# Moving the start of the activation rows from byte 128 to byte 0 of 512 in SBUF

## The chip, the cores and the metric

The kernel runs on one core of a Trainium2 chip. Its time is the device time of one execution in microseconds. Before the change three executions took 1005.29, 1007.73 and 1007.76 us; the median is 1007.73 us.

## The reference, cut to what matters

Two transformer blocks work on 256 tokens of width 1024. The first has a windowed attention and a differential attention, both gated and merged, and then a feed-forward part; the second has a chunked delta rule and a sparse latent attention, then a cross attention over 256 memory rows, and again a feed-forward part. All is float32. The feed-forward part, which takes more time than any other, is

```
gate_up = u @ w_ffn_in[l]
f = (silu(gate_up[..., :D_FF]) * gate_up[..., D_FF:]) @ w_ffn_out[l]
```

with D_FF = 2816. The second one has `w_gate`, `w_up` and `w_down` in place of these. Nearly all other work of TensorE is a projection of the same kind: 256 tokens times a weight matrix of 1024 rows.

## The kernel before, in words

Activations stand with features on the 128 partitions and tokens along the row: a block of 128 features is one row segment of 256 float32 numbers, 1024 bytes in each partition. Every float32 operand of a projection is split into a high and a low part (`split`, L285 to L292 for activations, `load_w` for weights) that TensorE takes at the full rate of the rounded type. `gemm` (L314 on) makes one output block of 128 features: it loads 512 KB of weights, splits them on ScalarE (L309) and VectorE (L311) into `wh` and `wl`, and issues 24 matmuls at L325: for each of eight blocks `wh` with the high and with the low rows, and then `wl` with the high rows. Weights are stationary (128 columns, 512 bytes in a partition, loaded before every matmul while the one before it streams), the rows are moving (256 columns, 1024 bytes). Each matmul has its own weight load.

The moving rows of these matmuls are, in the order of the program:

- `uh`, `ul`: the normalized input of a projection. In the first block's attention (gates, queries, values; 768 matmuls of 256 columns and 240 of 272), in both feed-forward parts (`ffn_in`, 1056 each) and in the queries of the cross attention (192).
- `od_h`, `od_l` and `m_h`, `m_l`: 192 matmuls each, between the attention and the first feed-forward part.
- `mem_h`, `mem_l`: the memory rows, 192 matmuls with the rows moving, 192 (L821 to L823) with the rows stationary and the weights moving.
- `f_h`, `f_l`: the inside of the feed-forward part. In the first block 528 matmuls with the rows moving. In the second (`down`, L1650 to L1654) they are stationary, and the weights `wh`, `wl` move, in pieces of 512 and 256 columns; 330 matmuls.
- `mix_h`, `mix_l` and `ox_h`, `ox_l`: 192 matmuls each, in the two residual steps of the second block.

The tiles get their addresses from an allocator when the program is built. The start of each row segment, counted as its address modulo 512 bytes, is: `u`, `f`, `mix`, `ox`, `od`, `m` 128; `mem` 64; nearly all weights 64 (one of the last three `wh` of the second feed-forward part 192). A row segment of 256 numbers and a weight segment of 128 are whole multiples of 512 bytes, so all blocks of a tile start at the same byte. The table `AT` (L214) holds how many numbers a tile's first row is moved into its allocation; `rows_at`, `new_u_at` and `parts_at` (L415 to L425) use it. In the three `ffn_in` steps j = 3, 6 and 12 a matmul with a stationary block of zeros (L328) stands after the fourth matmul of the gate's `gemm`; it adds nothing to the sum.

The order of the work on each engine comes from a scheduler at build time.

Of the kernel before, what the change touches and what calls it, by code (L numbers as in the profile page):

```python
# [17 lines left out]
F32R = mybir.dt.float32r  # L18
# [7 lines left out]
P = 128  # L26
NT = 256
# [6 lines left out]
FT = FF // P  # L34
# [176 lines left out]
BDLAST = 0  # L211
WARM = 12

AT = {'ffn1': 112, 'xatt': 0, 'ffn2': 112, 'mem_h': 112, 'mem_l': 112, 'mix_h': 0, 'mix_l': 0, 'ox_h': 0, 'ox_l': 0, 'f': 0, 'first': 112}  # L214
RB = 2
MAGIC = float(0x5F3759DF)
SWAP = [i ^ 16 for i in range(32)]
# [4 lines left out]
def _program(tc, d, out):  # L222
# [4 lines left out]
    def new_pool(stack, name, bufs=1, space=None, side=None):  # L227
        kw = {} if space is None else {"space": space}
        if side is not None:
            kw["side"] = side  # L230
        return stack.enter_context(tc.tile_pool(name=name, bufs=bufs, **kw))

    with ctx:
# [189 lines left out]
        def parts_at(pool_, name, at_h, at_l):  # L423
            return [rows_at(pool_.tile([P, KT * NT + P], F32R, name=name + e), at)
                    for e, at in (("_h", at_h), ("_l", at_l))]  # L425
# [12 lines left out]
        uh, ul = ([t[:, at + k * 3 * P:at + k * 3 * P + NK] for k in range(KT)] for t, at in (  # L438
            (gpool.tile([P, KT * 3 * P + 112], F32R, name="u" + e, tag="u" + e), AT["first"] + (0, 16)[e == "l"])
            for e in "hl"))  # L440
# [6 lines left out]
        for k in range(1, KT, 2):  # L447
            n = min(2, KT - k)
# [321 lines left out]
        first = [None]  # L770
# [19 lines left out]
        mem_h = mhp.tile([P, 8, NT], F32R, name="mem_h")  # L790
        mem_l = mhp.tile([P, 8, NT], F32R, name="mem_l")
# [37 lines left out]
        mpool = new_pool(mg, "m")  # L829
# [24 lines left out]
        def post_norm(src_w, xs, gain, res, res_out, g_next, at=0, at_l=0, whole=False):  # L854

            fg = mpool.tile([P, 8, NT], F32, name="fg", tag="fg")
            acc = gpool.tile([P, NK], F32, name="acc", tag="acc", bufs=1)[:, :NT]
            for j in range(8):
                def use(o, j=j):
                    act.activation(fg[:, j, :], o, AF.Copy, scale=G(gain, j))  # L860
                    sumsq(j, o, acc, NT)
                gemm_long(src_w[j], xs, NT, use)
            rr = gpool.tile([P, NK], F32, name="rs", tag="rs", bufs=2)
            rsqrt_of(opool, acc, ones_d, NT, rr[:, :NT])
            if whole:
                u = gpool.tile([P, KT, NK], F32, name="u", tag="uh")
            else:
                uh, ul = new_u_at(at, at_l)
            acc2 = gpool.tile([P, NK], F32, name="acc2", tag="acc2", bufs=1)[:, :NT]
            for j in range(8):  # L870
                dve.tensor_tensor(fg[:, j, :], fg[:, j, :], rr[:, :NT], OP.mult)  # L871
                pool.tensor_tensor(res_out[:, j, :], fg[:, j, :], res[:, j, :NT], OP.add)
                if whole:
                    act.activation(u[:, j, :NT], res_out[:, j, :], AF.Copy, scale=G(g_next, j))
                else:
                    split(uh[:, j, :NT], ul[:, j, :NT], res_out[:, j, :], G(g_next, j))
                sumsq(j, res_out[:, j, :], acc2, NT)
            rs2 = gpool.tile([P, NK], F32, name="rs", tag="rs", bufs=2)
            rsqrt_of(opool, acc2, ones_d, NT, rs2[:, :NT])
            if whole:  # L880
                return [u[:, k, :NT] for k in range(8)], rs2[:, :NT]
            return [(uh[:, k, :NT], ul[:, k, :NT]) for k in range(8)], rs2[:, :NT]

        h1 = rpool.tile([P, KT, NT], F32, name="h1", tag="resB")
        us, rs = post_norm(d["w_out1"], [(m_h[:, k, :], m_l[:, k, :]) for k in range(8)],
                           "post_mix", hT, h1, "pre_ffn", at=AT["ffn1"], at_l=AT["ffn1"] + 16)

        def ffn_in(pool_, src_w, us, rs, f_h, f_l):
            zeros = pool_.tile([96, P], F32R, name="zeros")
            pool.memset(zeros.bitcast(F32), 0.0)  # L890
            for j in range(FT):
                sg = pool_.tile([P, NT], F32, name="sg", tag="sg", bufs=3)

                def use_g(o, sg=sg):
                    dve.tensor_tensor(sg, o, rs, OP.mult)  # L895
                    act.activation(sg, sg, AF.Silu)  # L896
                    pool.tensor_tensor(sg, sg, rs, OP.mult)  # L897

                def use_u(o, sg=sg, j=j):
                    t = pool_.tile([P, NT], F32, name="ft", tag="ft", bufs=2)  # L900
                    dve.tensor_tensor(t, o, sg, OP.mult)  # L901
                    split(f_h[:, j, :], f_l[:, j, :], t)

                bank = lambda i: ppool.tile([P, 512], F32, name="s", tag="s") if 2 * j + i < 3 else None
                gemm(src_w[2 * j], us, NT, use_g, ps=bank(0), zero=zeros if j in (3, 6, 12) else None)
                gemm(src_w[2 * j + 1], us, NT, use_u, ps=bank(1))
            tc.keep_in_program_order(act.preload_act_table_set(EXP_LN))
# [20 lines left out]
        late(cc, d["const_c"])  # L928
        fst = ExitStack()
        mpool = new_pool(fst, "f")  # L930
        f_h = mpool.tile([P, FT, NT], F32R, name="f_h")
        f_l = mpool.tile([P, FT, NT], F32R, name="f_l")
        ffn_in(mpool, d["w_gu1"], us, rs, f_h, f_l)
        s = ppool.tile([P, 512], F32, name="s", tag="s")
        pe.matmul(s[:8, :384], relb, cc, start=True, stop=True)
# [39 lines left out]
        dve.memset(ones_q, 1.0 / 256)  # L975
        mix_h, mix_l = parts_at(bpool, "mix", AT["mix_h"], AT["mix_l"])

# [561 lines left out]
        def residual(src_w, xs, res, res_out, g_next, late=(), more=0, at=0):  # L1539
            uh, ul = new_u_at(at, at)  # L1540
            acc = gpool.tile([P, NK], F32, name="acc", tag="acc", bufs=1)[:, :NT]
            for j in range(8):
                def use(o, j=j):
                    dve.tensor_tensor(res_out[:, j, :], o, res[:, j, :], OP.add)
                    added.append(split(uh[:, j, :NT], ul[:, j, :NT], res_out[:, j, :], G(g_next, j)))
                    sumsq(j, res_out[:, j, :], acc, NT)
                ps = ppool.tile([P, 512], F32, name="s", tag="s") if 2 <= j < 2 + more else None
                gemm(src_w[j], xs, NT, use, ps=ps, late=late if j < 2 + more else ())
            rs2 = gpool.tile([P, NK], F32, name="rs", tag="rs", bufs=2)
            rsqrt_of(opool, acc, ones_d, NT, rs2[:, :NT])  # L1550
            return [(uh[:, k, :NT], ul[:, k, :NT]) for k in range(8)], rs2[:, :NT]

        x2 = rpool.tile([P, KT, NT], F32, name="x2", tag="resB")
        us, rs = residual(d["w_out2"], [(mix_h[:, k, :], mix_l[:, k, :]) for k in range(8)], x1, x2, "g_xattn", (0,1,2,3), 2, AT["xatt"])
        b2.close()
# [7 lines left out]
        def two(name, src):  # L1563
            h, l = (xpool.tile([P, 2, NT], F32R, name=name + e, tag=name + e, bufs=2) for e in "hl")
            with tc.issue_after(added[1].ins):
                act.activation(h, src, AF.Copy)
            pool.tensor_tensor(l, src, h.bitcast(F32), OP.subtract)
            return h, l
        keys = [two("kx_", kx[:, 2 * h:2 * h + 2, :]) for h in range(4)]
        values = [two("vx_", vx[:, :, h * NT:(h + 1) * NT]) for h in range(4)]  # L1570
        ox_h, ox_l = parts_at(xpool, "ox", AT["ox_h"], AT["ox_l"])
        rx = xpool.tile([P, 4], F32, name="rx")
# [45 lines left out]
        x3 = rpool.tile([P, KT, NK], F32, name="x3", tag="resA")[:, :, :NT]  # L1618
        us, rs = residual(d["w_xo"], [(ox_h[:, k, :], ox_l[:, k, :]) for k in range(8)], x2, x3, "g_ffn", (4,5,6,7), 2, AT["ffn2"])
        xa.close()  # L1620
# [4 lines left out]
        mpool = new_pool(fst, "f2")  # L1625
# [4 lines left out]
        for qb in range(2):  # L1630
# [5 lines left out]
        f_h, f_l = (mpool.tile([P, FT * NT + P], F32R, name=n)[:, AT["f"]:AT["f"] + FT * NT].rearrange(  # L1636
            "p (a b) -> p a b", a=FT) for n in ("f_h", "f_l"))
# [31 lines left out]
        for qb in range(2):  # L1669
# [13 lines left out]
            a = mpool.tile([P, 1], F32, name="ra", tag="ra", bufs=2)  # L1683
            b = mpool.tile([P, 1], F32, name="rb", tag="rb", bufs=2)
# [31 lines left out]
```

## Time and profile before

| | |
|---|---|
| median of three executions | 1007.73 us |
| the profiled execution's own time | 1007.77 us |
| its span, first to last instruction | 1005.9 us |
| TensorE busy (PE) | 982.8 us, 98% |
| weight loads (PEld), beside PE | 915.2 us, 91% |
| VectorE (DVE), ScalarE (ACT), GpSimd (POOL) busy | 685.1, 541.3, 222.8 us |
| mean granted TensorE clock | 0.993 |

A matmul's record in this profile is longer than the time that it holds up the next one (the engine is a pipeline): what it costs is the distance from its start to the start of the next. That distance is read from the timeline, or from a piece of the chain of waits, in which a run of matmuls is one row with its duration and count.

### The profile page before, as it was taken

What the parts mean: (1) busy time and instruction counts of PE and PEld (TensorE: products, weight loads), DVE (VectorE), ACT (ScalarE), POOL (GpSimd) and SP (SyncE); (2) the same over time, 40 slices, a digit from 0 to 9 for tenths busy, and PEclk for the clock granted to TensorE, in tenths of its full rate; (3) what the DMA queues carried; (4) which work ended last, traced back from release to release, by engine and by line L of the source; (5) the groups of instructions that cost most, each with busy time, mean ns of one, the idle gap of its engine ahead of it and who ended that gap; (6) DMA issues with size and microseconds to landing.
All of it is one profiled execution on the core that took longest, in us unless ns stands there. A gap on an engine that the chain in (4) does not pass through costs nothing.

```text
span 1005.9 us, 18620 instructions
## 1 busy us (share of the span) xinstructions
PE 982.8 (98%) x7218; PEld 915.2 (91%) x7218; DVE 685.1 (68%) x1466; ACT 541.3 (54%) x1097; POOL 222.8 (22%) x258
## 2 busy tenths in 40 slices
PE   9999999999999999999999899999999999999996
PEld 8888898998988989999999888787799999999885
DVE  6788789788655776656544739967687686566534
ACT  5566657667545755555544444335676554444433
POOL 5534326233230213121100312121021011212002
PEclk9999999999999999999999999999999999999999
DMA  6433333332435465555666232333056155555651
GB/s 238 151 110 104 123 126 106 106 126 87 165 120 194 148 210 199 186 184 187 211 199 195 85 127 84 126 105 105 1 167 203 70 181 185 185 186 189 208 189 64
DMA packets 42023, 149.26 MB, mean 148 GB/s; under 512 B 4728, under 2 KB 5376, under 8 KB 41808
## 3 DMA queue, kind: packets, MB, share of 16 engines
q1 hardware_dynamic: 40896, 145.47, 43.8%
q0 software_dynamic: 608, 2.03, 0.7%
q8 instruction: 56, 0.92, 0.4%
q10 hardware_dynamic: 432, 0.59, 0.2%
q14 instruction: 31, 0.25, 0.1%
HBM read 147.01 MB, written 1.06 MB: 147 GB/s over the span
## 4 chain that ended last, share of the span: by engine, by line
PE 57%; DVE 9%; ACT 2%; issue 1%; ACTq 0%; DVEq 0%
PE mm L325 36%; PE mm L341 4%; PE s L325 2%; PE ac L1653 2%; PE ac L1654 2%; PE ac L1650 2%; DVE wl L311 1%; DVE fg L871 1%; PE mm L1413 1%; PE mm L823 1%; DVE ul L292 1%; PE mm L821 1%; PE mm L822 1%; DVE y L1014 1%; DVE base L1158 0%
## 5 line engine op out<-in xcount | busy, mean ns | idle before, releaser
L311 DVE TENSOR_TENSOR wl<-raw,wh 128x1024 fp32r<-128x1024 f32 (+1 forms) x232 | 285.0, 1229 | 101.1 <-ACT wh L309 94.3
L309 ACT ACTIVATE wh<-raw 128x1024 fp32r<-128x1024 f32 (+1 forms) x232 | 242.8, 1048 | 175.0 <-PE mm L325 100.9
L325 PE MATMUL mm<-uh,wh 128*128 128x256 f32 (+1 forms) x1040 | 257.6, 284 | 0.0
L325 PE MATMUL mm<-ul,wh 128*128 128x256 f32 (+1 forms) x1040 | 255.8, 282 | 0.4 <-DVE ul L292 0.4
L325 PEld LDWEIGHTS mm<-uh,wh 128*128 128x128 f32 x1040 | 195.3, 188 | 2.8 <-ACT wh L309 0.6
L325 PEld LDWEIGHTS mm<-ul,wh 128*128 128x128 f32 x1040 | 195.3, 188 | 1.2 <-DVE ul L292 0.8
L325 PE MATMUL mm<-uh,wl 128*128 128x256 f32 (+1 forms) x1040 | 152.2, 283 | 0.0
L325 PEld LDWEIGHTS mm<-uh,wl 128*128 128x128 f32 x1040 | 134.6, 188 | 0.8
L341 PE MATMUL mm<-u,raw 128*128 128x256 f32 (+1 forms) x464 | 109.3, 386 | 0.0
L897 POOL TENSOR_TENSOR sg<-sg,rs 128x256 f32<-128x256 f32 x44 | 50.7, 1154 | 232.1 <-ACT sg L896 232.1
L341 PEld LDWEIGHTS mm<-u,raw 128*128 128x128 f32 x464 | 85.5, 190 | 14.0 <-issue 0.9
L901 DVE TENSOR_TENSOR ft<-mm,sg 128x256 f32<-128x256 f32 x42 | 17.8, 424 | 50.8 <-PE mm L325 49.6
L325 PE MATMUL mm<-f_h,wh 128*128 128x256 f32 x176 | 42.5, 279 | 0.0
L325 PE MATMUL mm<-f_l,wh 128*128 128x256 f32 x176 | 42.5, 279 | 0.0
L895 DVE TENSOR_TENSOR sg<-mm,rs 128x256 f32<-128x256 f32 x40 | 16.9, 423 | 32.2 <-PE mm L325 32.2
L288 ACT ACTIVATE f_h<-ft 128x256 fp32r<-128x256 f32 x44 | 18.3, 417 | 38.1 <-DVE ft L901 38.1
L1653 PE MATMUL ac<-wh,f_l 128*128 128x512 f32 (+1 forms) x110 | 38.3, 349 | 0.0
L1650 PE MATMUL ac<-wh,f_h 128*128 128x512 f32 (+1 forms) x110 | 38.3, 348 | 0.0
L1654 PE MATMUL ac<-wl,f_h 128*128 128x512 f32 (+1 forms) x110 | 38.0, 349 | 0.0
L896 ACT ACTIVATE sg<-sg 128x256 f32<-128x256 f32 x44 | 18.1, 417 | 33.4 <-DVE sg L895 33.4
L325 PEld LDWEIGHTS mm<-f_l,wh 128*128 128x128 f32 x176 | 33.0, 188 | 0.0
L325 PEld LDWEIGHTS mm<-f_h,wh 128*128 128x128 f32 x176 | 33.0, 188 | 0.0
(545 smaller groups left out, 2104.7 us busy)
## 6 DMA issues: line engine op xcount, KB each, us to landing
raw<-w_gu SPq DMA_DIRECT2D x88, 512.0 KB, 4.1
raw<-w_dn SPq DMA_DIRECT2D x22, 512.0 KB, 4.3
raw<-w_pr SPq DMA_DIRECT2D x20, 512.0 KB, 3.4
raw<-w_gate SPq DMA_DIRECT2D x16, 512.0 KB, 3.5
raw<-w_out SPq DMA_DIRECT2D x16, 512.0 KB, 3.6
raw<-w_fo SPq DMA_DIRECT2D x16, 512.0 KB, 3.5
raw<-w_kb SPq DMA_DIRECT2D x8, 512.0 KB, 3.5
raw<-w_vb SPq DMA_DIRECT2D x8, 512.0 KB, 3.5
```

What stands on the lines that cost most here:

```text
L288: m = act.activation(h, src, AF.Copy)
L309: act.activation(h[:, :kt * c], raw[:, :kt * c], AF.Copy)
L311: eng.tensor_tensor(l[:, :kt * c], raw[:, :kt * c], h[:, :kt * c].bitcast(F32), OP.subtract)
L325: pe.matmul(o, w[:, k * P:(k + 1) * P], xs[k][i], start=(first and n_ == 0), stop=(last and n_ == len(steps) - 1))
L341: pe.matmul(o, raw[:, k * P:(k + 1) * P], x, start=(k == 0), stop=(k == len(xs) - 1))
L895: dve.tensor_tensor(sg, o, rs, OP.mult)
L896: act.activation(sg, sg, AF.Silu)
L897: pool.tensor_tensor(sg, sg, rs, OP.mult)
L901: dve.tensor_tensor(t, o, sg, OP.mult)
L1650: m = pe.matmul(o, f_h[:, k, tok], h[:, cols], start=(k == 0), stop=False)
L1653: pe.matmul(o, f_l[:, k, tok], h[:, cols], start=False, stop=False)
L1654: pe.matmul(o, f_h[:, k, tok], l[:, cols], start=False, stop=(k == FT - 1))
```

## The change

The table `AT` gets new numbers, and the tiles `f_h` and `f_l` of the first block get the same form as those of the second: a tile that is 128 numbers longer, whose rows begin `AT["f"]` numbers into it. With the allocator's addresses, which stay where they were, every row segment of `u`, `f`, `mix` and `ox` now begins at byte 0 of 512. Rows of `od`, `m` and `mem` and all weights begin where they did. The number and the order of the instructions on each engine are the same before and after.

```
-AT = {'ffn1': 112, 'xatt': 0, 'ffn2': 112, 'mem_h': 112, 'mem_l': 112, 'mix_h': 0, 'mix_l': 0, 'ox_h': 0, 'ox_l': 0, 'f': 0, 'first': 112}
+AT = {'ffn1': 80, 'xatt': 96, 'ffn2': 80, 'mix_h': 96, 'mix_l': 96, 'ox_h': 96, 'ox_l': 96, 'f': 96, 'first': 80}
...
-        f_h = mpool.tile([P, FT, NT], F32R, name="f_h")
-        f_l = mpool.tile([P, FT, NT], F32R, name="f_l")
+        f_h, f_l = (mpool.tile([P, FT * NT + P], F32R, name=n)[:, AT["f"]:AT["f"] + FT * NT].rearrange(
+            "p (a b) -> p a b", a=FT) for n in ("f_h", "f_l"))
```

## Rows read from the trace of the kernel before

**Rows 1.** The page: busy time of each engine, share, instructions; granted clock in tenths

```profile
PE 982.8 (98%) x7218; PEld 915.2 (91%) x7218; DVE 685.1 (68%) x1466; ACT 541.3 (54%) x1097; POOL 222.8 (22%) x258
...
PEclk9999999999999999999999999999999999999999
```

**Rows 2.** PE by stage: stretch, its length, busy (records), granted clock, DMA

```profile
0.00:312.00 312.00, 307.32 (x2146) 1.00 0.40 133
...
396.00:548.00 152.00, 152.00 (x1293) 1.00 0.60 193
...
816.00:936.00 120.00, 120.00 (x1020) 1.00 0.57 185
```

**Rows 3.** The chain of waits: start us, us, what, how many

```profile
375.55 3.38 PE mm L325 x28
...
379.04 16.96 PE mm L325 x144
396.13 33.92 PE mm L325 x288
430.16 118.25 PE mm L325 x1004
...
846.48 33.92 PE mm L325 x288
880.52 56.06 PE mm L325 x476
```

**Rows 4.** Timeline of PE, mix rows: start us, us, line, operation, out<-in

```profile
729.08 0.28 PE L325 MATMUL mm<-mix_h,wh 128*128 128x256 f32 x1
...
729.99 0.62 PE L325 MATMUL mm<-mix_h,wl 128*128 128x256 f32 x4
```

**Rows 5.** Timeline of PE, mem rows

```profile
339.08 0.28 PE L325 MATMUL mm<-mem_h,wh 128*128 128x256 f32 x1
...
341.00 1.12 PE L325 MATMUL mm<-mem_h,wl 128*128 128x256 f32 x8
```

**Rows 6.** Timeline of PE, second block's down stage, f stationary

```profile
941.30 0.28 PE L1650 MATMUL ac<-wh,f_h 128*128 128x256 f32 x1
...
942.01 0.39 PE L1650 MATMUL ac<-wh,f_h 128*128 128x512 f32 x1
...
944.11 0.28 PE L1650 MATMUL ac<-wh,f_h 128*128 128x256 f32 x1
...
944.79 0.39 PE L1650 MATMUL ac<-wh,f_h 128*128 128x512 f32 x1
```

**Rows 7.** Timeline of PE, u rows, beginning of the first ffn_in

```profile
375.70 0.28 PE L325 MATMUL mm<-ul,wh 128*128 128x256 f32 x1
...
377.40 1.07 PE L325 MATMUL mm<-uh,wl 128*128 128x256 f32 x8
```

**Rows 8.** The chain of waits from 333 to 380 us: the matmul with zeros

```profile
378.93 0.12 PE mm L328
```

**Rows 9.** Groups of PE by shape: record's mean length in ns last before the bar

```profile
L325 PE MATMUL mm<-f_h,wl 128*128 128x256 f32 x176 | 24.6, 279 | 0.0
...
L325 PE MATMUL mm<-mem_h,wl 128*128 128x256 f32 x64 | 9.0, 283 | 0.0
...
L325 PE MATMUL mm<-mix_h,wl 128*128 128x256 f32 x48 | 6.7, 276 | 0.0
```

**Rows 10.** The page: weight splits (group, mean ns), and the weights' DMA

```profile
L311 DVE TENSOR_TENSOR wl<-raw,wh 128x1024 fp32r<-128x1024 f32 (+1 forms) x232 | 285.0, 1229 | 101.1 <-ACT wh L309 94.3
L309 ACT ACTIVATE wh<-raw 128x1024 fp32r<-128x1024 f32 (+1 forms) x232 | 242.8, 1048 | 175.0 <-PE mm L325 100.9
...
raw<-w_gu SPq DMA_DIRECT2D x88, 512.0 KB, 4.1
```

**Rows 11.** Waits of PE: who waited for whom, us in total, times, longest

```profile
PE mm L823 <- DVE wl L311: 4.5, 2, 3.9
```

## The prediction

> **What bounds the kernel now.** I read the page first. TensorE is busy for 98% of the span and its clock stands in the page's top tenth in all 40 slices [rows 1], so neither a cold clock nor an idle TensorE leaves much to win. Then the waits of TensorE: the longest sum is 4.5 us, two waits for VectorE's split of a memory weight [rows 11]. Then the stages: TensorE is busy for 307.32 of the first 312 us, and for every microsecond from 396 to 548 and from 816 to 936 [rows 2]. The chain of waits confirms it: there it is one unbroken run of matmuls at L325 [rows 3]. In these stretches the kernel's time is the number of matmuls times the distance between two starts. A change that alters neither number nor order of instructions can act only through that distance.
>
> So I asked what the distance is. In the feed-forward parts it is 118.25 us / 1004 = 117.78 ns, and 33.92 us / 288 = 117.78 ns in both blocks, to the hundredth [rows 3]. These are `u` and `f` rows at byte 128 with weights at byte 64. The same shape runs at other rates elsewhere:
>
> - `mem` rows, byte 64 like the weights: 16 distances from 339.08 to 341.00 us, 120.0 ns [rows 5].
> - `mix` rows, byte 128: eight distances from 729.08 to 729.99 us, 113.8 ns, and nearer 113.3 if more are counted (the times are rounded to 10 ns) [rows 4].
> - `u` rows at the start of the first `ffn_in`: 15 distances from 375.70 to 377.40 us, 113.3 ns [rows 7]. Then comes the matmul with zeros, a stationary block at another place [rows 8], and the next 144 take 16.96 us, 117.8 ns each [rows 3].
>
> The lengths of the records say the same: 276, 279 and 283 ns for `mix`, `f` and `mem` [rows 9]. So with 64 bytes between rows and weights two rates are stable, 113.3 and 117.8 ns. A run keeps its rate until something interrupts it, and what begins or interrupts it chooses. With 0 bytes between them I see only 120.0. [...]
>
> [...]
>
> **The change part by part.** Moved are the rows of 3 x (1024 + 80) = 3312 `u` matmuls, 528 `f`, 192 `mix` and 192 `ox`: 4224 in all. They go from 64 bytes ahead of the weights to 64 bytes behind them. The trace has no moving row at byte 0 with weights at byte 64 in a long run. The nearest rows with 64 bytes behind are those of the second block's down stage, where the weights move (byte 64) and `f` is stationary (byte 128). In its runs of six matmuls of 256 columns both rates appear in turn: from 941.30 to 942.01 us six take 0.71 us, 118 ns, and from 944.11 to 944.79 us six take 0.68 us, 113 ns [rows 6]. [...] That is my nearest row: the same two rates, about as often the one as the other, none above.
>
> What a full move to the fast rate is worth: 117.78 - 113.33 = 4.45 ns a matmul.
>
> - First feed-forward part: 1056 + 528, less 27 that are fast already [rows 7]: 1557. Second: 1056. All on the unbroken chain: 2613 x 4.45 ns = 11.6 us.
> - First attention: (768 + 240) x 4.45 ns = 4.5 us. TensorE is busy there but shares the time with work that waits for VectorE and ScalarE, so I count half as reaching the end, 2.2 us.
> - Cross attention: 192 `u` + 192 `ox`, 384 x 4.45 ns = 1.7 us, counted by half likewise, 0.9 us.
> - `mix`: fast already; nothing to win, and 192 x 4.45 ns = 0.9 us to lose.
> - Down stage: the pair turns round, 64 behind becomes 64 ahead. Its nine pieces of 512 columns take 2.10 us (942.01 to 944.11), 233 ns each [rows 6]. I count it as nothing; if its 132 matmuls of 256 columns went all fast or all slow it would be 132 x 2.2 ns = 0.3 us either way.
>
> All fast: 11.6 + 2.2 + 0.9 = 14.7 us, or 17.8 us if nothing in the attentions is hidden, which gives 1007.8 - 17.8 = 990.0 us, the lower end. From the down stage I take half of 14.7 us, 7.35, less half of the loss of `mix`, 0.45: 6.9 us. All this is counted against the profiled execution, 1007.77 us with a span of 1005.9; it lies 0.04 us from the median of the three runs. 1007.8 - 6.9 = 1000.9; I say 1000.9 us. The half is not a mean over thousands of draws: the two long stretches are one run of matmuls each, so I expect mostly one rate in each of them, and a step of about 7 us (first) or 4.7 us (second) where it is the fast one.
>
> What follows behind a faster TensorE has room: in 24 x 113.3 ns = 2.72 us a `gemm` needs 1.05 us of ScalarE and 1.23 us of VectorE for its weights, and 512 KB in 2.72 us is 193 GB/s, which the stretch from 396 to 548 us moves already [rows 2]; a load lands in 4.1 us with three buffers [rows 10].
>
> **The rivals.**
>
> *All slow.* The new place has the same two rates, but the beginnings choose the slow one everywhere. For it: with 64 bytes ahead that is what both long stretches do, and only `mix` and a few short runs do otherwise [rows 3, 4]. Against it: the down stage takes turns. `mix` loses 0.9 us and the fast 27 lose 0.1: 1008.8 us, no change that can be told.
>
> *No effect of the place.* The rates are a matter of timing alone; then the same beginnings choose the same rates: 1007.8 us. Against it stand the 120.0 ns that `mem` has throughout [rows 5]. [...]
>
> [...]
>
> **How the numbers follow.** What a measurement can tell from no change here is 0.3%, 3.0 us. Forecast, some of the long stretches fast: 0.52, with its own range 990 to 1004.7 us. All slow 0.17 and no effect 0.09: together 0.26 for no change. Meeting at once, or another rate over 118.9: 0.22, from 1010.8 to 1018 us. The range that leaves out two in ten goes from 991 us, just above the lower end, to 1013 us, into the third rival.
>
> **What would show it.** Right: the runs of L325 in the chain from 379 to 548 us and from 829 to 936 us at 113.3 ns a matmul, in one of them at least; records of 276 ns in the groups of `f` or `u`; the `mem`, `od` and `m` groups as before. The down stage shows whether the pair turned round keeps its two rates. [...] I would be wrong altogether if a fourth rate appeared, below 113 or over 121 ns, or if the time changed where no rows were moved.

## The result, and the profile after

The kernel with the moved rows takes 993.4 us (median of four executions, 991.37 to 994.63), the kernel before 1007.75 us in the same comparison: ratio 0.9859, interval [0.9834, 0.9884]. A second comparison gave 993.32 us (five executions), ratio 0.9855 [0.9832, 0.9879]. So the change wins 14.4 us where I had forecast 6.9.

The page of the profiled execution (991.37 us, span 989.5 us) has the busy times and the granted clock in tenths, as [rows 1]:

```profile
PE 966.0 (98%) x7218; PEld 899.2 (91%) x7218; DVE 685.9 (69%) x1466; ACT 541.8 (55%) x1097; POOL 223.2 (23%) x258
...
PEclk9999999999999999999999899999999999999999
```

TensorE is busy for the same share of a shorter span; instructions and the other engines' work are what they were. The chain of waits through the second feed-forward part answers to the row of 288 at 846.48 us in [rows 3]; its columns are start, length, what, how many:

```profile
834.42 32.66 PE mm L325 x288
```

32.66 us / 288 = 113.4 ns from start to start, where it was 117.78. In the first feed-forward part the timeline shows the same; the rows are the eight matmuls of `wl` that end a `gemm`, and one matmul with zeros:

```profile
374.68 1.07 PE L325 MATMUL mm<-uh,wl 128*128 128x256 f32 x8
...
388.28 1.07 PE L325 MATMUL mm<-uh,wl 128*128 128x256 f32 x8
...
389.64 0.29 PE L328 MATMUL mm<-ul,zeros 96*128 96x256 f32 x1
...
391.14 1.07 PE L325 MATMUL mm<-uh,wl 128*128 128x256 f32 x8
...
393.86 1.07 PE L325 MATMUL mm<-uh,wl 128*128 128x256 f32 x8
```

From 374.68 to 388.28 us are five `gemm`s, 120 matmuls in 13.60 us: 113.3 ns. The `gemm` with the zeros takes 2.86 us, the next one 2.72 again. Before the change the first of these matmuls ended the 113.3 ns for good [rows 7, 8]; now the rate survives it. By tile (count, record length in ns as min/median/max, first and last start), the rows of `f`:

```profile
L325 PE MATMUL mm<-f_h,wl x176: 276/276/276, 478.3 to 536.2; 128*128 128x256 f32 x176
```

The same view of `m`:

```profile
L325 PE MATMUL mm<-m_h,wl x64: 276/276/276, 310.7 to 328.9; 128*128 128x256 f32 x64
```

And of `mix`:

```profile
L325 PE MATMUL mm<-mix_h,wl x48: 281/281/281, 717.5 to 737.4; 128*128 128x256 f32 x48
```

`f` went from 279 to 276 [rows 9], the length that goes with 113.3 ns. But `mix`, 276 before [rows 9], is now at 281, 117.8 ns from start to start, and `m`, whose place did not change, is at 276 where it was 279. The down stage, as in [rows 6]:

```profile
939.51 0.28 PE L1650 MATMUL ac<-wh,f_h 128*128 128x256 f32 x1
...
940.20 0.39 PE L1650 MATMUL ac<-wh,f_h 128*128 128x512 f32 x1
...
942.25 0.28 PE L1650 MATMUL ac<-wh,f_h 128*128 128x256 f32 x1
...
942.93 0.39 PE L1650 MATMUL ac<-wh,f_h 128*128 128x512 f32 x1
```

Every run of six now takes 0.68 to 0.69 us, where 0.71 and 0.68 took turns, and nine pieces of 512 columns take 2.05 us, 228 ns each (228.9 over more of them), where they took 233.

Where the time came from, by the starts of stages in three profiled executions (us; the second profile after is e12 below). The long run of an `ffn_in` is its part without a gap; 120 of the first one's 1056 matmuls and 44 of the second one's stand ahead of it.

| stretch | before | after | after, second profile |
|---|---|---|---|
| start to first matmul of `m` | 306.0 | 304.5 | 305.3 |
| from there to the long run of the first `ffn_in` | 69.4 | 65.4 | 67.7 |
| from there to the last `f` matmul | 172.7 | 166.4 | 166.4 |
| from there to the next block's first run of 32 matmuls at L341 | 27.3 | 28.0 | 28.5 |
| from there to the long run of the second `ffn_in` | 241.3 | 241.4 | 241.2 |
| from there to the end | 189.2 | 183.8 | 183.8 |
| span | 1005.9 | 989.5 | 992.7 |

The long feed-forward stretches are shorter by a fixed amount, 6.3 and 5.4 us, and the first attention by 0.8 to 1.6. The second and the fourth line differ between the two executions of the same kernel, and the granted clock (the number behind TensorE's busy time and its records) shows why. First the second line, before, after and second profile (columns as in [rows 2]):

```profile
306.00:375.40 69.40, 66.10 (x512) 0.95 0.57 189
...
304.50:369.80 65.30, 62.26 (x512) 1.00 0.63 201
...
305.30:372.90 67.60, 64.54 (x512) 0.97 0.61 194
```

And the fourth:

```profile
548.20:575.40 27.20, 23.34 (x166) 0.94 0.29 98
...
536.30:564.20 27.90, 24.05 (x166) 0.88 0.30 97
...
539.30:567.70 28.40, 24.54 (x167) 0.88 0.30 95
```

By half microseconds, the granted clock in these stretches is 0.50 in place of 1.00 for some time: before the change from 313.5 to 316.5, 358.0 to 361.0 and 566.0 to 569.0 us, in the first profile after it from 552.5 to 559.0 us. Ahead of each TensorE waits (it is busy for 0.50 of the 2 us from 310.0, 0.86 of those from 354.0, 0.01 of those from 562.0 and, after the change, 0.10 of those from 550.0), but not every wait brings it: after the change TensorE is busy for 0.82 of the 2 us from 350.0, and the clock stays at 1.00. In the second line that can cost up to 69.4 x 0.05 = 3.5 us before the change, 67.6 x 0.03 = 2.0 in the second profile after, and nothing in the first (estimates from these rows): of the 4.0 and 1.8 us that are gone there, up to 3.5 and 1.5 come from the clock and not from the change. In the fourth the same matmuls keep TensorE busy 0.7 and 1.2 us longer, and by just that the stretch grew; the 8 among the nines of the page stands for it.

### The profile page after: what moved, and what is told of

It is laid out like the page before. It is cut to its first block, busy times and chain, and to the rows that moved or that the text cites. A ratio compares the mean times of both kernels' runs of the same rounds, so it can differ in the third digit from the quotient of the medians.

```text
span 989.5 us, 18620 instructions
## 1 busy us (share of the span) xinstructions
PE 966.0 (98%) x7218; PEld 899.2 (91%) x7218; DVE 685.9 (69%) x1466; ACT 541.8 (55%) x1097; POOL 223.2 (23%) x258
## 5 line engine op out<-in xcount | busy, mean ns | idle before, releaser
L325 PE MATMUL mm<-uh,wh 128*128 128x256 f32 (+1 forms) x1040 | 251.7, 282 | 0.0
L325 PE MATMUL mm<-ul,wh 128*128 128x256 f32 (+1 forms) x1040 | 249.5, 280 | 0.8 <-DVE ul L292 0.8
L325 PEld LDWEIGHTS mm<-uh,wh 128*128 128x128 f32 x1040 | 195.5, 188 | 2.8 <-ACT wh L309 0.6
L325 PEld LDWEIGHTS mm<-ul,wh 128*128 128x128 f32 x1040 | 195.7, 188 | 1.4 <-DVE ul L292 1.0
L325 PE MATMUL mm<-uh,wl 128*128 128x256 f32 (+1 forms) x1040 | 148.9, 280 | 0.0
L325 PEld LDWEIGHTS mm<-uh,wl 128*128 128x128 f32 x1040 | 131.7, 188 | 0.8 <-issue 0.2
L341 PE MATMUL mm<-u,raw 128*128 128x256 f32 (+1 forms) x464 | 109.3, 386 | 0.0
L341 PEld LDWEIGHTS mm<-u,raw 128*128 128x128 f32 x464 | 85.5, 190 | 14.0 <-issue 0.9
L325 PE MATMUL mm<-f_l,wh 128*128 128x256 f32 x176 | 41.1, 276 | 0.0
L325 PE MATMUL mm<-f_h,wh 128*128 128x256 f32 x176 | 41.1, 276 | 0.0
L514 POOL TENSOR_TENSOR ropem<-rawq,cqt 128x256 f32<-128x256 f32 x16 | 18.9, 1179 | 64.6 <-ACT rawq L511 64.5
L325 PEld LDWEIGHTS mm<-f_l,wh 128*128 128x128 f32 x176 | 33.0, 188 | 0.0
```

Of the source, the lines that this page charges most:

```text
L325: pe.matmul(o, w[:, k * P:(k + 1) * P], xs[k][i], start=(first and n_ == 0), stop=(last and n_ == len(steps) - 1))
L341: pe.matmul(o, raw[:, k * P:(k + 1) * P], x, start=(k == 0), stop=(k == len(xs) - 1))
L514: pool.tensor_tensor(m[:, :n], raw[:, :n], c, OP.mult)
```

## The experiments

In the expectations, distance is the start of the moving rows less that of the stationary block: before the change 64 (ahead), after it -64 (behind). Theory A: the place sets the odds with which a run of matmuls takes one of two rates, and the run keeps its rate until something interrupts it. Theory B: the place alone decides. Theory C: the timing of the beginning alone.

| run | what | us | ratio to before |
|---|---|---|---|
| e1 | rows at byte 64 | 1015.19 | 1.0092 [1.0062, 1.0122] |
| e2 | only `u` at byte 0 | 996.69 | 0.9901 [0.9879, 0.9924] |
| e3 | zero matmul's block taken from `w` | 1006.75 | 1.0001 [0.9984, 1.0017] |
| e6 | rows at byte 256 | 991.12 | 0.9845 [0.9823, 0.9866] |
| e7 | after, `mem` at byte 0 too | 991.25 | 0.9853 [0.9831, 0.9875] |
| e8 | after, run of `mix` broken | 993.74 | one execution |
| e9 | only `f` at byte 0 | 1007.85 | 0.9993 [0.9978, 1.0009] |
| e10 | e9, run of `f` broken | 1005.08 | one execution |
| e11 | e7, run of `mix` broken | 990.87 | 0.9841 [0.9818, 0.9863] |
| e12 | after, again | 993.32 | 0.9855 [0.9832, 0.9879] |

### e1: the rows at the same byte as the weights

```
-AT = {'ffn1': 80, 'xatt': 96, 'ffn2': 80, 'mix_h': 96, ... 'f': 96, 'first': 80}
+AT = {'ffn1': 96, 'xatt': 112, 'ffn2': 96, 'mix_h': 112, ... 'f': 112, 'first': 96}
```

> The kernel after with the rows of u, f, mix and ox at byte 64, the byte at which the weights begin. Three theories. A (place sets the odds): with a given distance between rows and weights certain rates are stable, a run keeps its rate until something interrupts it, and the distance sets which rate its beginning falls into. B (place alone): each distance has one rate, whatever went before. C (timing alone): the place is indifferent. A and B expect 120.0 ns a matmul in both long stretches, as the mem rows have it at this distance, and about 1018 us (4032 matmuls x 2.2 ns and 192 x 6.7 ns over 1007.8). C expects 113.3 or 117.8 ns and 991 to 1008 us.

It took 1015.19 us. The stretches of the first and second feed-forward part (columns: stretch, length, PE busy with its number of records, granted clock, DMA share, GB/s) show fewer matmuls at the same clock:

```profile
400.00:430.00 30.00, 30.00 (x252) 1.00 0.58 190
...
840.00:900.00 60.00, 60.00 (x502) 1.00 0.58 185
```

The changed kernel has 267 and 531 records in these stretches. Less the two or three in flight at the edges, 252 in 30 us are 120.0 ns each. So 120.0 ns a matmul was right for distance 0, though the time stayed 2.8 us under the 1018 us expected; 64 behind, the changed kernel's long runs have 113.4. C is out: with the same beginnings the place moved the time by 21.8 us.

### e2: `u` alone

```
-... 'mix_h': 96, 'mix_l': 96, 'ox_h': 96, 'ox_l': 96, 'f': 96, ...
+... 'mix_h': 0, 'mix_l': 0, 'ox_h': 0, 'ox_l': 0, 'f': 0, ...
```

> Only the rows of u begin at byte 0; f, mix and ox are back at byte 128. A: gates and ups of both feed-forward parts at 113.4 ns as after; the f run of the first part follows without an interruption and keeps 113.3 ns although its rows lie at byte 128; the second part's down stage takes turns again (six in 0.685 and 0.707 us); about 994.5 us. B: u at 113.4 ns, f and ox back at 117.8 ns, mix at 113.3 ns: 993.4 + 528 x 4.45 ns + 192 x 4.45 ns - 192 x 4.45 ns + 1 = 996.8 us. C: any mixture of the two rates.

It took 996.69 us. `u` runs at 113.5 ns; `f`, 64 ahead as before the change, is at 117.8 from its first matmul, right behind `u` at 113.5:

```profile
L325 PE MATMUL mm<-f_h,wl x176: 278/280/281, 481.5 to 541.7; 128*128 128x256 f32 x176
```

B's number held, in part by luck: it counted `mix` at 113.3 ns, and `mix` ran at 117.8 here (median record 280 ns). A's, that 113.3 ns go on at the other distance, did not: `f` at 64 ahead dropped them at the border, though nothing stands between.

### e3: does the zero block's place end the 113.3 ns?

```
-                    pe.matmul(o, zero, xs[k][i][:96], start=False, stop=False)
+                    pe.matmul(o, w[:96, k * P:(k + 1) * P], xs[k][i][:96], start=False, stop=False)
```

> The kernel before (rows at byte 128) with one thing changed: the six extra matmuls at L328 take their stationary block from the weights at byte 64 (96 of their rows) in place of the block of zeros at byte 256 or 128; so what they add to the sum is not zero. Order and count of instructions stay. A: the first of them no longer interrupts the fast run that begins at 375.5 us; the first feed-forward part keeps 113.3 ns, 1557 x 4.45 ns = 6.9 us less: 1000.9 us; the second part, which begins slow, stays slow. If it is not the block's place but its 96 rows that interrupt, or under B, nothing changes: 1007.8 us.

In this kernel, the one before but for that block (which adds to the sum, as the zeros did not), the timeline at the first extra matmul reads:

```profile
376.41 1.07 PE L325 MATMUL mm<-uh,wl 128*128 128x256 f32 x8
...
377.77 0.28 PE L328 MATMUL mm<-ul,wh 96*128 96x256 f32 x1
...
379.31 1.10 PE L325 MATMUL mm<-uh,wl 128*128 128x256 f32 x8
```

Eight matmuls of `wl` take 1.07 us before it, 1.10 behind it, as before the change. So A's expectation failed: that it is another matmul ends the run, not where its block lies. And `mix`, at 113.3 ns in the kernel before (276 in [rows 9]), ran at 117.8 ns here with nothing of it changed: the first sign that its rate is drawn anew.

```profile
L325 PE MATMUL mm<-mix_h,wl x48: 277/279/281, 727.5 to 747.4; 128*128 128x256 f32 x48
```

### e4: the distances by themselves

A program of matmuls alone: for each of twelve distances twelve runs of 40, each run behind a float32 matmul of another width.

```
for diff in (-256, -192, -128, -96, -64, -32, 0, 32, 64, 96, 128, 192):
    for e in range(64, 256, 16):
        matmul(st[:, :e], one[:, :P], one[:, :e])
        for n in range(40):
            matmul(acc[:, :256], block n % 8 of wts, block n % 8 of rows)   # rows start diff bytes after wts
```

> A kernel that does none of the reference's work and measures the disputed cost alone: weights at byte 64, rows at twelve distances from them (-256, -192, -128, -96, -64, -32, 0, 32, 64, 96, 128, 192 bytes, in this order), at each twelve runs of 40 matmuls of 128 x 256 of the rounded type, eight blocks in turn; ahead of each run a float32 matmul of 64 to 240 columns, so that the runs begin at different phases. A: 120.0 ns at distance 0; at +64 both 113.3 and 117.8 ns with most runs slow, at -64 both with most runs fast; elsewhere unknown. B: one rate at each distance, 117.8 at +64, 113.3 at -64, 120.0 at 0. C: the same rates at every distance.

One run of 40 of six of the distances from the chain (-256, -192, -64, 0, 64 and 192; start, length):

```profile
60.17 4.79 PE acc L258 x40
...
120.32 4.71 PE acc L258 x40
...
299.41 4.56 PE acc L258 x40
...
419.74 4.79 PE acc L258 x40
...
539.38 4.71 PE acc L258 x40
...
719.19 4.56 PE acc L258 x40
```

-64 and 192 have the shortest, 4.56 / 40 = 114.0 ns with the longer first distances in it and 113.33 behind them; 64 and -192 have 4.71, 117.8; 0 and -256 have 4.79, 120.0 behind the first. The other six take 4.67 to 4.79. Distances 256 apart agree, -128 and 128 (4.75 both) too. At -64 all twelve runs settle at 113.33, at 64 all twelve at 117.78; there the place alone decided, and the even odds of my forecast are gone. Not so everywhere: at -96 the runs settle at 117.2 to 120.0 ns, and at -128 and 128 single ones at 120.1 and the others at 118.8.

### e5: beginnings, orders and other bytes

A second program of this kind; its core, for each of -64 and 64:

```
for c in (31, 45, ... 241):                     # 16 runs of 40 that wait for VectorE
    tensor_copy(o32[:, :c], acc[:, :c]); run(40)
for g in range(6): gemm order, wts/wts2 with rows/rows2, unbroken
for weights at byte 128, 192, 320: 3 runs of 32
for g in range(8): down order: 9 of 512 columns, 6 of 256, two stationary blocks in turn (a, b, a)
```

> A program that does none of the reference's work: only matmuls of 128x256 (and some of 128x512) with a weight load each, clocked by their starts. It asks whether the rate belongs to the distance between the start of the moving rows and that of the weights alone. Theory P (the distance alone, as the first such program showed: 64 bytes behind 113.3 ns, 64 ahead 117.8 ns, whatever comes before): (1) 32 runs of 40 that each begin after a wait for VectorE of another length: 113.3 at 64 behind in all 16, 117.8 at 64 ahead in all 16; (2) the order of a gemm, each weight block twice and two tiles of rows, six gemms unbroken: the same two rates; (3) weights at bytes 128, 192 and 320 with the rows 64 behind or ahead: the same two rates; (4) the order of the down stage, in which each matmul has another stationary block and the moving operand stays for two: the same two rates in its six-runs of 256, so 64 behind 113.3 and 64 ahead 117.8. Theory Q (something else of the sequence decides, as `mix`, 64 behind, runs at 117.8 in the changed kernel, and the down stage, 64 ahead there, at 113.3): some of the 16 runs after a wait go to the other rate, or the order of the down stage turns the two round.

From the chain, four runs that began after a wait (the first two at -64, the next two at 64), the `gemm` order (-64, then 64) and the down order (-64, then 64):

```profile
38.27 4.99 PE acc L262 x40
...
69.79 4.82 PE acc L262 x40
...
133.12 4.99 PE acc L262 x40
...
165.61 4.82 PE acc L262 x40
...
181.53 16.40 PE acc L279 x144
...
198.10 17.01 PE acc L279 x144
...
286.14 22.39 PE acc L294 x120
...
308.69 21.99 PE acc L294 x120
```

After a wait both rates appear at both distances: 4.99 us is a run that settled at 117.8 ns, 4.82 one at 113.3 (the first two intervals, in which it starts up, take 0.34 us). At -64, 13 of 16 settle at 113.3 ns (of the other three, the program's first took 7.05 us), at 64 3 of 16. In the `gemm` order -64 has 113.3 ns and 64 117.8; at other bytes of the weights 8 of 9 and 0 of 9 have 113.3. Over both programs, -64 settles at 113.3 ns in 34 of 38 beginnings (12, 13, 1 and 8) and 64 in 3 of 38. So P's rule is a matter of odds, as A has it, but far from even.

The odds belong to these programs and to how a run begins. Behind another matmul -64 took 113.3 ns in 21 of 22 beginnings and 64 in none of 22; behind a wait it was 13 and 3 of 16. In the kernels the six extra matmuls of L328 agree: behind each of them `u` has 113.3 ns in the seven profiles with `u` at -64 or 192 (after, e2, e6, e7, e8, e11, e12) and 117.8 in the four at 64 (before, e3, e9, e10). Two beginnings don't agree. The first 28 of the long run of the first `ffn_in` have 113.3 ns at 64 too, in all four profiles [rows 7]. And `mix`, which begins behind a wait, has 113.3 ns in one of five profiles at 64 (before; not e2, e3, e9, e10) and in one of five at -64 or 192 (e12; not after, e6, e7, nor e8 ahead of its break): its distance made no difference.

The down order turns it round: at 64 its runs of six are all at 113.3 ns, at -64 they take turns at 113.3 and 117.7 by the starts of single records, just as in [rows 6], in all eight rounds, the same each time. What I had read as odds is the pattern of another order. (Its three matmuls have two stationary blocks, a, b, a; the expectation's "another stationary block" for each doesn't hold between the third and the next.)

### e6: byte 256

```
-AT = {'ffn1': 80, 'xatt': 96, 'ffn2': 80, 'mix_h': 96, ... 'f': 96, 'first': 80}
+AT = {'ffn1': 16, 'xatt': 32, 'ffn2': 16, 'mix_h': 32, ... 'f': 32, 'first': 16}
```

> The rows of u, f, mix and ox begin at byte 256 of 512, 192 ahead of the weights. If the places repeat every 256 bytes, as 192 ahead and 64 behind both ran at 113.3 ns in the program that measured the distances, this is the changed kernel again: 993.4 us, first and second feed-forward part at 113.4 ns. If what counts is nearness in a segment of 512 bytes (rows and weights within 64 bytes or not), 192 ahead has nothing to do with 64 behind in a kernel whose tiles take turns, and the time lies anywhere between 993 and 1015 us.

991.12 us, and the changed kernel's number of records in the same stretch:

```profile
400.00:430.00 30.00, 30.00 (x267) 1.00 0.59 193
```

192 ahead is as good as 64 behind, in the kernel too: with the four pairs of e4, all that was tried speaks for the distance modulo 256 bytes.

### e7: the memory rows as well

```
-        mem_h = mhp.tile([P, 8, NT], F32R, name="mem_h")
+        mem_h = rows_at(mhp.tile([P, KT * NT + P], F32R, name="mem_h"), 112)
```

(and `mem_l` alike.)

> The changed kernel with the memory rows, too, at byte 0 (they were at byte 64, like the weights): 192 matmuls in which they move should go from 120.0 to 113.3 ns, 1.3 us; 192 in which they are stationary and the weights move come to 64 bytes ahead: 117.8 ns by the program that measured the distances (0.4 us), 113.3 by the down stage of the changed kernel (1.3 us). From 993.4 us that makes 990.8 to 991.7 us if nothing else is late there; if VectorE's split of the weights, for which TensorE waits 3.9 us in that stage, takes it back, 993.4 us.

```profile
L325 PE MATMUL mm<-mem_h,wl x64: 276/276/383, 333.5 to 361.4; 128*128 128x256 f32 x64
L821 PE MATMUL mm<-wh,mem_h x64: 276/279/469, 540.3 to 653.9; 128*128 128x256 f32 x64
```

The median is 276 where the rows move (283 in [rows 9]) and 279 where they are stationary (L821; 283 before): the rule carries over to rows that the change left alone. The time, 991.25 us, is within the spread of the changed kernel's executions; a gain of 1.7 us can't be told from none.

### e8: break the run of `mix`

The fourth matmul of three of its `gemm`s is done in two halves:

```
-                pe.matmul(o, w[:, k * P:(k + 1) * P], xs[k][i], ...)
+                for c in ((slice(0, P), slice(P, n)) if cut and n_ == 3 else (slice(0, n),)):
+                    pe.matmul(o[:, c], w[:, k * P:(k + 1) * P], xs[k][i][:, c], ...)
```

> The changed kernel; in the residual step with mix, three of the eight gemms (the third, fifth and seventh) do their fourth matmul in two halves of 128 columns, which breaks the run of equal matmuls. In the changed kernel mix runs at 117.8 ns, 196 matmuls in a row, though its rows stand 64 bytes behind the weights. Theory A, as it now stands (the distance sets the odds with which a run takes one of two rates, here about nine to one for 113.3, and it keeps the rate until something interrupts it): mix goes to 113.3 ns after the first break or the second, and stays there; up to 0.7 us. Rival D (something of mix itself, the place of its weights or of its sums, makes it slow): 117.8 ns after all three breaks, and the time as that of the changed kernel.

```profile
726.09 0.63 PE L326 MATMUL s<-mix_h,wl 128*128 128x256 f32 x4
...
727.50 0.63 PE L326 MATMUL s<-mix_h,wl 128*128 128x256 f32 x4
...
729.74 0.33 PE L326 MATMUL mm<-mix_l,wh 128*128 128x128 f32 x2
...
731.35 1.07 PE L326 MATMUL mm<-mix_h,wl 128*128 128x256 f32 x8
...
734.07 1.07 PE L326 MATMUL mm<-mix_h,wl 128*128 128x256 f32 x8
```

The statement of L325 stands on L326 in this kernel. Ahead of the break twelve matmuls take 1.41 us (117.5 ns), behind it 24 take 2.72 (113.3), and so it stays to the end of `mix`. D is out, and what A says of a break holds in this execution; the nine in ten that it names for a beginning are not what `mix` shows (e5).

### e9 and e10: `f` alone, and its run broken

e9 is the kernel before with the longer `f` tiles of the change and

```
-AT = {... 'f': 0, ...}
+AT = {... 'f': 96, ...}
```

e10 adds the halves of e8 to three of the output blocks of `f`:

```
-                gemm_long(src_w[j], xs, NT, use)
+                gemm_long(src_w[j], xs, NT, use, cut=whole and j in (1, 3, 5))
```

> Only the f rows of the first block, and with them the stationary f of the down stage, begin at byte 0; u, mix and ox stay at byte 128. If the distance decides for each kind of rows by itself: f at 113.3 ns, 528 x 4.45 = 2.3 us; the down stage, whose moving weights then stand 64 ahead of f, as in the changed kernel, at 113.3 and 228.9 ns, 0.7 + 0.3 = 1.0 us; u as before; sum 3.3 us, 1003.0 us against 1006.3. If f takes the rate over from u, which runs at 117.8 ns before it: only the down stage gains, 1005.3 us.

> The kernel in which f alone begins at byte 0, with three matmuls of its first-block product (the fourth of the second, fourth and sixth output block) done in two halves of 128 columns. With f alone moved, f ran at 117.8 ns from its first matmul on, though it stands 64 bytes behind the weights; just before it u runs at 117.8 ns without a gap. Theory A (a run keeps the rate that it entered with, until something breaks it; at 64 behind a new beginning takes 113.3 about nine times in ten): 117.8 ns for 69 matmuls, then 113.3 ns from the first break or the second on, 450 matmuls x 4.45 ns = 2.0 us. Rival D (something of f itself, once u stands elsewhere): 117.8 ns throughout.

e9 took 1007.85 us. Its `f`, 64 bytes behind the weights, is at 117.9 ns, entered straight from `u` at that rate (24 matmuls from row to row: 2.83 us):

```profile
493.01 1.10 PE L325 MATMUL mm<-f_h,wl 128*128 128x256 f32 x8
...
495.84 1.10 PE L325 MATMUL mm<-f_h,wl 128*128 128x256 f32 x8
```

In e10 the same `f` has 117.8 ns for its first 69 matmuls and 113.3 from the first break on:

```profile
491.77 0.87 PE L326 MATMUL mm<-f_h,wl 128*128 128x256 f32 x6
...
492.83 0.33 PE L326 MATMUL mm<-f_l,wh 128*128 128x128 f32 x2
...
494.42 1.07 PE L326 MATMUL mm<-f_h,wl 128*128 128x256 f32 x8
...
497.14 1.07 PE L326 MATMUL mm<-f_h,wl 128*128 128x256 f32 x8
```

So the good place alone isn't enough: a stretch at 117.8 ns keeps that on it until it is broken. Of the two readings of e9 the second held, without even its 1.0 us from the down stage: that runs at the changed kernel's distance, but entered from `u` at 117.8 ns its six-runs stay at 118.0 ns and its 512-column pieces at 230.2, by the starts of single records. With the same distance as in the changed kernel, what stands before the stage differs, and so does its rate.

### e11 and e12: all together, and the change once more

e11 is e7 with two halves in `mix`; e12 the changed kernel itself.

> The changed kernel with mem at byte 0 as well and with two breaks (a matmul in two halves) in the first and the fifth gemm of the step with mix: the sum of what the runs so far point to. mem as in the run with mem alone; mix at 113.3 ns from the first break on, up to 0.8 us. Against the changed kernel in the same call: 1 to 2.5 us less, if nothing else is late there.

> The changed kernel once more, on the same chip as the run before it: 993.4 us, and the second comparison with the kernel before. Every theory expects the rates of the first profile in the two feed-forward parts (113.4 ns); mix and m, which start after a wait, may have taken the other rate.

990.87 and 993.32 us on one chip, 989.67 to 993.40 and 989.88 to 994.59: the difference points the expected way and isn't settled. In e11 the rates are as expected: 276 ns of record for the moving rows of `mem` and for `mix`, in the median. In e12, the same program as the changed kernel, two tiles took the other rate than in the first profile:

```profile
L325 PE MATMUL mm<-m_h,wl x64: 278/279/281, 311.6 to 330.4; 128*128 128x256 f32 x64
```

That is `m`, back at 279; and `mix`, back at 276:

```profile
L325 PE MATMUL mm<-mix_h,wl x48: 276/276/277, 721.1 to 740.2; 128*128 128x256 f32 x48
```

Both begin behind a wait. What they draw differs from execution to execution; `u` and `f` had 113.3 to 113.5 ns in both.

## Why the prediction had the direction right and the size wrong

**What bounds the kernel** was right: number and order of instructions stayed, the mean granted clock nearly so (0.993 before, 0.995 and 0.993 after), and the time went by the distance of two starts.

**Two rates, and a run keeps its rate until something interrupts it**: right, shown by e8 and e10, where a break alone changes the rate, and by e12 against the first profile. One limit: 117.8 ns passed from `u` to `f` (e9), 113.3 ns at 64 behind did not pass to `f` at 64 ahead (e2).

**The failed step is "From the down stage I take half of 14.7 us".** The down stage was the only place with 64 bytes behind [rows 6], but there the weights move and the stationary blocks come in another order. Its two rates take turns by that order (e5), not by even odds. In the order of a `gemm`, e5 has 113.3 ns at 64 behind, unbroken, and in e4 and e5 together 34 of 38 beginnings of all kinds have it. Both long runs went wholly to 113.4 ns, not half of them: 10.7 us where the half had 5.8, and the time moved by 14.4 us in place of 6.9.

**The other terms.** That my sum for "all fast", 14.7 us, comes so near to 14.4 is partly luck, since its terms missed both ways. The long runs: 11.6 us counted, 6.3 + 4.4 = 10.7 measured; I had counted all of each `ffn_in` to the unbroken chain, but the first four of [rows 3] add up to 1464 matmuls with `f`, not 1584. First attention: 2.2 counted, 0.8 to 1.6 gained. Down stage: counted as nothing, gained 61.3 - 60.3 = 1.0 us by the starts of its first and last matmul; I had weighed its 256-column runs and not the nine pieces of 512. `mix`: 0.45 lost by count (half of 0.9), 0.8 or nothing by its first and last start, as it has 117.8 or 113.3 ns. Cross attention: 0.9 counted, 0.2 to 0.6 gained. What the low clock takes, up to 3.5 us ahead of the first long run, stands in no term; it differs between executions of one kernel, and one profile can't tell it from a gain.

**The rivals.** *No effect of the place* fell with e1 and with the result: the same loads take 113.3, 117.8 and 120.0 ns a matmul at three places (-64, 64 and 0 in e4). *All slow* is what a kernel gets whose run enters at 117.8 ns: e9 shows it for `f`. The 0.22 was for rates over 118.9 ns at 64 behind, up to the 1018 us of 120.0 ns: no run shows that there, where the runs had about 113.3 or 117.8 ns; 120.0 ns came at distance 0 (e1, e4).

**What stays open.** What makes the places differ, and why `mix` and the first 28 of the first long run don't go by the distance, no run shows. Nor did I try a distance between weights of different places in turn.

## What to carry to other kernels

Where TensorE runs without gaps, take the distance from start to start of equal matmuls, by place of both operands; if it differs for one shape, try the four places at steps of 64 modulo 256 bytes in a small program that has the kernel's own order of stationary and moving blocks, since another order turned the answer round; then count again in the kernel, since one of its stages didn't follow the small program. An alternation in a trace isn't a probability: look whether it repeats exactly. And a rate that a run carries along can be a matter of how it began, so at a good place a long stretch at the worse rate may be cured by one break; entering it from a better one did not help at a bad place (e2).

## What the runs showed of the hardware that I had not expected

- The start of the moving rows less that of the stationary block, modulo 256 bytes, moves a 128x256 float32r matmul with its own weight load between 113.3 (-64) and 120.0 ns (0), 6%, at a granted clock of 1.00 (e4).
- At one distance two rates are stable. A run of over a thousand matmuls kept 117.8 ns across output blocks and from `u` to `f`, in e9 from 64 ahead to 64 behind, and one matmul done in two halves changed it (e10).
- The same program drew other rates for `m` and `mix` in two executions: 276 against 279, and 281 against 276 ns of record length.
- How a run begins weighs as much as its place: behind another matmul 113.3 ns came in 21 of 22 beginnings at -64 and in none of 22 at 64, behind a wait in 13 and 3 of 16 (e4, e5), and for `mix` in one of five profiles at either.
